# A two-layer decoder trunk on one core: the norm's sums one unit later, one mean by VectorE, and single PSUM tiles in two places

## The chip, the core and the metric

The kernel runs on one core of a Trainium2 chip. The metric is the device time of one execution in microseconds (us). The engines are named as the profile names them: PE (TensorE) with its weight loads PEld, DVE (VectorE), ACT (ScalarE), POOL (GpSimd), SP (SyncE, which here only issues DMAs).

## The reference

256 tokens of width 2048 in float32 pass two layers. Each layer is a mixer and a gated feed-forward net (FFN), each followed by a layer norm over a scaled residual:

```python
for i in range(DEPTH):                       # 2 layers
    if i < N_A_LAYERS:
        mix = pool_mixer(h, pool_w_in[i], pool_w_grp[i], pool_scale[i], pool_w_out[i])
    else:
        if i == N_A_LAYERS:                  # shared keys and values from the stream after layer 0
            k_shared = (h @ shared_w_k)...; v_shared = (h @ shared_w_v)...
        mix = dilated_attention(h, k_shared, v_shared, attn_w_q[j], attn_w_o[j])
    h = layer_norm(DEEPNORM_ALPHA * h + mix, ln1_g[i], ln1_b[i])
    ff = conv_ffn(h, ffn_w_up[i], ffn_conv_w[i], ffn_conv_b[i], ffn_w_down[i])
    h = layer_norm(DEEPNORM_ALPHA * h + ff, ln2_g[i], ln2_b[i])
```

`layer_norm` subtracts the mean over the 2048 features, divides by the root of the variance and applies a gain and an offset per feature.

## The kernel before

**Units.** All weights pass once through the core as blocks of 512 x 512 (128 partitions x 4 row chunks x 512 columns), 1 MB each, some of 384 rows. One block is one entry of the list `units`. `run_units` goes through that list: for unit i it first issues loads up to unit i + 5 and the splits up to unit i + 3 (`ahead`), then runs what `before[i]` holds, then emits the unit's matmuls, then the actions of `pending` that are due, then the unit's `post`, where it is the last of a group. `later(n, fn)` puts an action behind the matmuls of the n-th next unit. Each engine works through its own instructions in the order of emission, so this hand-written order decides what waits behind what.

**Splitting.** Weights and activations are float32. A block is split into a rounded part `wh` (ACT, line 99) and the rest `wl` (DVE, line 100), four buffers of each; a raw block has three buffers, so the load of unit u starts when unit u - 3 is split. The first four units are split in four pieces each. Activations are kept in tiles of quarters: `XC[q]` holds the high and the low part of quarter q of the features (512 of 2048), `H[q]` the float32 stream. The matmuls multiply high by high, high by low and low by high.

**PSUM.** One pool gives all accumulators: four tiles of two banks (`pair`); `bank` takes a pair's first half only. The framework puts in the semaphores. It orders the accesses of different engines to one PSUM tile.

**The start.** `x_quad(q)` transposes quarter q of x by eight matmuls into one pair, one bank for each half of the quarter, then for each half ACT copies the high part and DVE subtracts to get the low part; one ACT copy of both banks to `H[q]` follows in the unit after. Quarters 1 to 3 are transposed in the middle of units 0 to 2.

**The norm after the first FFN.** `add_last` multiplies by the down projection in four column groups c = 0 to 3; `resid_last` adds each group's result to `H[c]`. When H[0] is complete, a quarter of its mean-like sum is used as a shift (`shift`), which is taken off every quarter, so that the variance can be taken from sums of squares: H[0] by DVE in `one`, H[1] to H[3] by accumulating DMAs that POOL issues (`less`). `stats` and `folds` then sum each quarter and its square into `ST["S"]` and `ST["Q"]`; `xp(q)` makes `XP[q]`, the quarter times the gain and not yet normalised. `chain` has PE sum S and Q over the partitions (lines 429 and 430), then computes the inverse deviation and, one step per unit, normalises the quarters (`norm`), applies gain and offset (`affine`) and makes the high and low parts (`lo`, line 305) that become `XC[q]`.

**What follows that norm.** Twelve units for the first four heads: four units of keys, which read `XP[q]` and are corrected afterwards by the mean and deviation (`norm_evac`, two units behind the last of them), four units of queries, which read `XC[0]` to `XC[3]` in turn, four units of values. The order of `later` numbers in `chain` and in `qk_post` decides in which order these steps stand on ACT and DVE.

**The end of the attention.** `outputs(hq, ms)` multiplies two heads' values by their transposed probabilities into one pair, and ACT and DVE make the two parts that the output projection reads; for the last group of heads (hq = 3) they do so head by head.

Of the kernel before, what the change touches and what calls it, by code (L numbers as in the profile page):

```python
# [9 lines left out]
F32 = mybir.dt.float32  # L10
# [3 lines left out]
OP = mybir.AluOpType  # L14
# [3 lines left out]
T = 256  # L18
P = 128
# [13 lines left out]
def trunk(ctx: ExitStack, tc: tile.TileContext, x, pool_w_in, pool_w_grp, pool_scale, pool_w_out,  # L33
# [3 lines left out]
    V, A, PE = nc.vector, nc.scalar, nc.tensor  # L37
# [10 lines left out]
    def pair(nm):  # L48
        return psp.tile([P, 2, 512], F32, name=nm, tag="ps")

    def bank(nm):
        return pair(nm)[:, 0, :]

    def pairs(ps, n=4):
        return [(m, min(2, n - m), ps[m].both) for m in range(0, n, 2)]
# [16 lines left out]
    pending, before = [], {}  # L72
# [62 lines left out]
    def later(n, fn):  # L135
        if n == 0:
            fn()
        else:
            pending.append([n, fn])
# [158 lines left out]
    def w4(nm):  # L298
        return lnp.tile([P, 4, T], F32, name=nm, tag="w4")
# [15 lines left out]
    H, XC, XP, ST = {}, {}, {}, {}  # L315
    vec, cvec, gbx = [], [], {}
    ident = const.tile([P, P], F32, name="ident")
# [13 lines left out]
    def resid_last(c, first, lay, which, after):  # L331
        def post(ps):
            for m, n, p in pairs(ps):
                y = H[c][:, m:m + n, :]
                if first and c == 0:
                    V.scalar_tensor_tensor(y, y, ALPHA, p[:, :, :T], op0=OP.mult, op1=OP.add)
                else:
                    V.tensor_tensor(y, y, p[:, :, :T], OP.add)
                if c < 3:
                    V.tensor_tensor(y, y, p[:, :, T:], OP.add)  # L340
                else:
                    square(3, m)
            if c == 0:
                ST["w4"] = w4("fold")
                s = fold(H[0], None, "S0", F32R)
                later(1, lambda: shift(s, first, lay, which))
            elif c < 3:
                n = 3 if c == 1 and not first else 1
                later(n, lambda: stats(c))
                later(n + 1, lambda: xp(c, lay, which))  # L350
            else:
                folds(3)
                xp(3, lay, which)
                later(1, lambda: chain(ps[0], lay, which, after))
        return post

    def square(q, m):
        if m == 0:
            ST["sq"] = lnp.tile([P, 4, T], F32, name="sq", tag="sq")
        A.activation(ST["sq"][:, m:m + 2], H[q][:, m:m + 2], AF.Square)  # L360

    def fold(src, acc, nm, dt=F32):
        t2, t1 = ST["w4"][:, 0:2, :], ST["w4"][:, 2, :]
        V.tensor_tensor(t2, src[:, 0:2, :], src[:, 2:4, :], OP.add)
        if acc is None:
            t1 = lnp.tile([P, T], dt, name=nm, tag=nm[0])
        V.tensor_tensor(t1, t2[:, 0, :], t2[:, 1, :], OP.add)
        if acc is None:
            return t1
        V.tensor_tensor(acc, acc, t1, OP.add)  # L370
        return acc

    def folds(q):
        ST["S"] = fold(H[q], ST["S"], "S")
        ST["Q"] = fold(ST["sq"], ST["Q"], "Q")

    def stats(q):
        square(q, 0)
        square(q, 2)
        folds(q)  # L380

    def shift(s, first, lay, which):
        ps = bank("shift")
        PE.matmul(ps[:, :T], ones4, s, start=True, stop=True)
        if first:
            cs = ST["w4"][:, 3:4, :]
        else:
            cs = pools["ffn"].tile([P, 2, T], F32, name="cs", tag="xs", bufs=1)[:, 0:1, :]
        A.activation(cs[:, 0, :], ps[:, :T], AF.Copy, scale=-1.0)
        cb = cs.to_broadcast([P, 4, T])  # L390
        ST["S"] = ST["Q"] = None

        def one():
            V.tensor_tensor(H[0], H[0], cb, OP.add)
            if first:
                pre(1)
            stats(0)

        def two():
            xp(0, lay, which)  # L400
            if first:
                pre(2)
                pre(3)

        def pre(q):
            V.scalar_tensor_tensor(H[q], H[q], ALPHA, cb, op0=OP.mult, op1=OP.add)

        def less(q):
            nc.gpsimd.dma_start(H[q], cb, accum_op=OP.add)

        later(1, one)
        later(2, two)
        if not first:
            for q in (1, 2, 3):
                less(q)

    def xp(q, lay, which):
# [10 lines left out]
    def chain(ps, lay, which, after):  # L428
        PE.matmul(ps[:, :T], onesd, ST["S"], start=True, stop=True)
        PE.matmul(ps[:, T:], onesd, ST["Q"], start=True, stop=True)  # L430
        rm = lnp.tile([P, 4, T], F32, name="rm", tag="sq")
        rs, mr, var = rm[:, 0, :], rm[:, 1, :], rm[:, 2, :]
        ST["rs"], ST["mr"] = rm[:, 0:1, :], mr
        A.activation(rm[:, 3, :], ps[:, :T], AF.Square)
        V.tensor_tensor(var, ps[:, T:], rm[:, 3, :], OP.subtract)
        A.activation(var, var, AF.Sqrt, bias=epst)
        V.reciprocal(rs, var)
        V.tensor_tensor(mr, ps[:, :T], rs, OP.mult)
        mb, rb = rm[:, 1:2, :].to_broadcast([P, 4, T]), rm[:, 0:1, :].to_broadcast([P, 4, T])
        g0 = 32 * which  # L440

        def norm(q):
            V.tensor_tensor(H[q], H[q], rb, OP.mult)
            V.tensor_tensor(H[q], H[q], mb, OP.subtract)

        def affine(q):
            XC[q] = quad_tile("xc")
            for m in range(4):
                j = 4 * q + m
                A.activation(H[q][:, m, :], H[q][:, m, :], AF.Identity,  # L450
                             scale=vec[lay][:, g0 + j:g0 + j + 1], bias=vec[lay][:, g0 + 16 + j:g0 + 17 + j])
            A.copy(XC[q][:, :, 0, :T], H[q])

        def lo(q):
            lo_part(XC[q], H[q], 4)
            if after is not None:
                later((8, 11, 14, 17)[q], lambda: after(q))

        norm(0)
        for q in range(4):  # L460
            if q > 0:
                later(1 + q, lambda q=q: lo(q - 1))
            later(1 + q, lambda q=q: affine(q))
            if q < 3:
                later(1 + q, lambda q=q: norm(q + 1))
        later(5, lambda: lo(3))
# [69 lines left out]
    def x_quad(q, halves=(0, 1)):  # L536
        xin = XIN
        if halves[0] == 0:
            H[q] = hp.tile([P, 4, T], F32, name="h", tag="h")
            XC[q] = quad_tile("xc")  # L540
        if halves[0] == 0:
            ST["xT"] = pair("xT")
        both = ST["xT"]
        for half in halves:
            for kk in range(2):
                for t in range(2):
                    k = 2 * half + kk
                    PE.transpose(both[:, half, kk * T + t * P:kk * T + t * P + P], xin[q, t][:, k * P:(k + 1) * P],
                                 ident)
        for half in halves:  # L550
            pv2 = both[:, half, :].rearrange("p (k t) -> p k t", k=2)
            s = slice(2 * half, 2 * half + 2)
            A.copy(XC[q][:, s, 0, :T], pv2)
            V.tensor_tensor(XC[q][:, s, 1, :T], pv2, XC[q][:, s, 0, :T].bitcast(F32), OP.subtract)
        if halves[-1] == 1:
            before.setdefault(min(q + 1, 3), []).append(
                lambda: A.copy(H[q], both.rearrange("p b (k t) -> p (b k) t", k=2)))

    def add_in(g, mids=()):
        group(pool_w_in[0], rows4, 512 * g, 512, xsrcs, pool_post(g), mode="a" if g == 3 else "ab", mids=mids)  # L560
# [1 line left out]
    def add_grp(g):  # L562
# [12 lines left out]
             True, 0, 0, after=lambda q: to_tokens(q))  # L575
# [388 lines left out]
    qk, pr, oq, pT, vts = {}, {}, {}, {}, {}  # L964
# [140 lines left out]
    def outputs(hq, ms):  # L1105
        if ms[0] == 0:
            oq[hq] = quad_tile("o")
        vt = vts[hq]
        both = pair("o")
        for m in ms:  # L1110
            hd = slice(m * P, (m + 1) * P)
            ps = both[:, m % 2, :]
            t = pT.pop((hq, m))
            PE.matmul(ps[:, :T], vt[:, 0, hd], t[:, :T], start=True, stop=False)  # L1114
            PE.matmul(ps[:, P:T], vt[:, 1, hd], t[:, T:], start=False, stop=True)
        o = oq[hq][:, ms[0]:ms[0] + 2]
        for at in (slice(0, 1), slice(1, 2)) if hq == 3 else (slice(0, 2),):
            hi = o[:, at, 0, :T]
            A.copy(hi, both[:, at, :T])
            V.tensor_tensor(o[:, at, 1, :T], both[:, at, :T], hi.bitcast(F32), OP.subtract)  # L1120

    def v_group(hq):
        js = (0, 1, 2, 3)
# [18 lines left out]
    with tc.tile_pool(name="start", bufs=1) as stp:  # L1142
        one1 = stp.tile([P, P], F32, name="one1")
        for q in range(NQ):
            for t in range(2):
                XIN[q, t] = stp.tile([P, 512], F32, name=f"xin{q}{t}")
            halves = [slice(0, 256), slice(256, 512)] if q == 0 else [slice(0, 512)]
# [130 lines left out]
```

## Time and profile before

| | |
|---|---|
| median of 3 runs | 2023.74 us (2023.49 to 2025.34) |
| the profiled execution | 2024.98 us, its span 2023.2 us |
| instructions | 31428 |
| mean granted clock of PE | 0.999 |
| HBM read | 380.01 MB, 189 GB/s over the span |

The span runs from the first to the last instruction of the program. In the page's groups, in timelines and lists of waits, a line such as L100 is line 100 of the kernel; `out<-in` are the program's tile names; a bracket `[0.76 <-DVE xc L554]` is the time that the engine stood idle just before, and what ended it. Times in a timeline are us from the span's start, then the duration. An x and a number count instructions.

### The profile page before, as it was taken

The numbers are of one execution on the slowest core, as the hardware profiler recorded it, in microseconds if no ns is written. First come the engines' busy times: TensorE is split into PE (matmuls) and PEld (weight loads), VectorE is DVE, ScalarE is ACT, GpSimd is POOL, SyncE is SP. The second block draws the span as 40 slices with busy tenths as digits, with TensorE's granted clock in tenths as the row PEclk, the third lists the DMA queues.
The fourth block names the chain that finished last, engine by engine and source line by source line (L and its number), as shares of the span: only waits on it lengthen the run. The fifth ranks groups of instructions, "written<-read, shape, count | busy, mean of one in ns | idle before, by whom it ended". The sixth has DMA issues, their size and how long they took to land.

```text
span 2023.2 us, 31428 instructions
## 1 busy us (share of the span) xinstructions
PE 2011.6 (99%) x12742; PEld 1813.7 (90%) x12742; DVE 1728.5 (85%) x1822; ACT 1269.2 (63%) x1546; POOL 94.3 (5%) x154
## 2 busy tenths in 40 slices
PE   9999999999999999999999999999999999999999
PEld 8898988999899988888898988998899989989987
DVE  6868887999899999779796878787899899989898
ACT  5454686766766676656554444477767677667672
POOL 2000000000000000000000021000000000000000
PEclk9999999999999999999999999999999999999999
DMA  8565576676666767885565656557666757666765
GB/s 256 192 211 188 164 216 191 180 221 222 197 198 205 233 190 219 236 226 187 177 207 165 199 175 207 188 175 221 167 215 203 227 179 227 193 222 189 211 220 173
DMA packets 271825, 408.30 MB, mean 202 GB/s; under 512 B 74446, under 2 KB 86116, under 8 KB 271424
## 3 DMA queue, kind: packets, MB, share of 16 engines
q1 hardware_dynamic: 259488, 388.93, 59.1%
q0 software_dynamic: 11760, 16.70, 5.5%
q8 instruction: 100, 1.64, 0.3%
q10 hardware_dynamic: 432, 0.66, 0.1%
q14 instruction: 45, 0.37, 0.1%
HBM read 380.01 MB, written 2.10 MB: 189 GB/s over the span
## 4 chain that ended last, share of the span: by engine, by line
PE 98%; DVE 1%; DMA 0%; issue 0%; ACT 0%; SPq 0%; DVEq 0%
PE acc L180 44%; PE acc L181 22%; PE s L246 3%; PE s L244 3%; PE s L245 3%; PE acc L185 3%; PE t L246 2%; PE t L244 2%; PE t L245 2%; PE acc L184 2%; PE acc L183 2%; PE t L255 2%; PE t L257 2%; PE t L256 2%; PE s L1064 0%; PE o L1114 0%
## 5 line engine op out<-in xcount | busy, mean ns | idle before, releaser
L180 PE MATMUL acc<-xc,wh 128*128 128x512 f32 x3264 | 1151.8, 396 | 0.0
L181 PE MATMUL acc<-xc,wl 128*128 128x256 f32 x3264 | 916.0, 281 | 0.0
L100 DVE TENSOR_TENSOR wl<-raw,wh 128x2048 fp32r<-128x2048 f32 (+2 forms) x305 | 657.1, 2163 | 174.9 <-ACT wh L99 170.3
L180 PEld LDWEIGHTS acc<-xc,wh 128*128 128x128 f32 x3264 | 616.0, 189 | 143.3
L99 ACT CAST wh<-raw 128x2048 fp32r<-128x2048 f32 (+2 forms) x305 | 548.7, 1805 | 170.1 <-PE acc L180 70.4
L181 PEld LDWEIGHTS acc<-xc,wl 128*128 128x128 f32 x3264 | 615.4, 189 | 0.1
L113 ACT CAST wh<-raw 128x1024 fp32r<-128x1024 f32 x142 | 148.4, 1052 | 194.5 <-DVE raw L122 175.3
L114 DVE TENSOR_TENSOR wl<-raw,wh 128x1024 fp32r<-128x1024 f32 x142 | 169.4, 1221 | 11.2 <-ACT wh L113 11.2
L121 DVE TENSOR_TENSOR wl<-raw,wh 128x1536 fp32r<-128x1536 f32 x71 | 124.5, 1754 | 6.7 <-ACT wh L119 5.7
L119 ACT CAST wh<-raw 128x1536 fp32r<-128x1536 f32 x71 | 104.9, 1477 | 35.4 <-PE acc L180 28.2
L287 POOL DMA_DIRECT2D ht<-w x48 | 41.3, 1014 | 1446.7 <-DVE ht L877 722.1
L246 PE MATMUL t<-wh,g 128*128 128x256 f32 x376 | 105.7, 281 | 0.0
L244 PE MATMUL t<-wh,g 128*128 128x256 f32 x376 | 105.6, 281 | 0.0
L245 PE MATMUL t<-wl,g 128*128 128x256 f32 x376 | 105.4, 280 | 0.0
L620 ACT ACTIVATE c<-u,cv 128x256 f32<-128x256 f32 x172 | 89.5, 592 | 23.1 <-DVE f L682 16.6
L246 PE MATMUL s<-wh,xs 128*128 128x256 f32 x344 | 96.2, 280 | 0.0
L244 PE MATMUL s<-wh,xs 128*128 128x256 f32 x344 | 96.1, 279 | 0.0
L245 PE MATMUL s<-wl,xs 128*128 128x256 f32 x344 | 96.0, 279 | 0.0
L124 DVE TENSOR_TENSOR raw<-raw 128x1024 f32<-128x1024 f32 x71 | 87.0, 1225 | 2.4
L625 ACT ACTIVATE a<-u,cv 128x256 f32<-128x256 f32 x172 | 73.4, 499 | 11.9 <-DVE g L692 11.9
L611 ACT COPY u<-acc 128x512 f32<-128x512 f32 x84 | 46.9, 573 | 47.4 <-PE acc L181 47.1
L625 ACT ACTIVATE u<-u,cv 128x256 f32<-128x256 f32 x172 | 73.4, 499 | 0.0
(337 smaller groups left out, 3445.2 us busy)
## 6 DMA issues: line engine op xcount, KB each, us to landing
raw<-in_ffn_w_up_dram SPq DMA_DIRECT2D x160, 1024.0 KB, 5.2
raw<-in_ffn_w_down_dram SPq DMA_DIRECT2D x80, 1024.0 KB, 5.2
raw<-in_pool_w_out_dram SPq DMA_DIRECT2D x16, 1024.0 KB, 5.0
raw<-in_shared_w_k_dram SPq DMA_DIRECT2D x16, 1024.0 KB, 5.1
raw<-in_attn_w_q_dram SPq DMA_DIRECT2D x16, 1024.0 KB, 5.1
raw<-in_shared_w_v_dram SPq DMA_DIRECT2D x16, 1024.0 KB, 5.2
raw<-in_attn_w_o_dram SPq DMA_DIRECT2D x16, 1024.0 KB, 5.4
ht<-w POOLq DMA_DIRECT2D x50, 256.0 KB, 5.3
```

Source lines behind the costliest of these rows:

```text
L99: A.copy(wh[i][:, s], r[:, s])
L100: V.tensor_tensor(wl[i][:, s], r[:, s], wh[i][:, s].bitcast(F32), OP.subtract)
L113: A.copy(h[:, :, n], r[:, :, n])
L114: V.tensor_tensor(l[:, :, n], r[:, :, n], h[:, :, n].bitcast(F32), OP.subtract)
L119: A.copy(hs, rs)
L121: V.tensor_tensor(ls, rs, hs.bitcast(F32), OP.subtract)
L180: PE.matmul(ps[m].ap, h[:, k, c], q[:, k, :, :T], start=st, stop=False)
L181: PE.matmul(ps[m][:, :T], l[:, k, c], q[:, k, 0, :T], start=False, stop=sp)
L244: PE.matmul(to, xh, h[:, k, n], start=opens and kk == 0, stop=False)
L245: PE.matmul(to, xh, l[:, k, n], start=False, stop=False)
L246: PE.matmul(to, xl, h[:, k, n], start=False, stop=ends and kk == 1)
L625: A.activation(to[:, m, :], u[:, m, i:i + T], AF.Copy, scale=cv[:, i, j:j + 1])
```

## The change

- `resid_last`: for the norm after the first FFN, the only one with `first` false, `chain` is put behind the second unit after the sums are made, not behind the first. The steps that `chain` places by `later` move with it.
- `shift`: there, the shift of H[1] is added by a DVE instruction in `one`, behind that of H[0]; `less` issues DMAs for H[2] and H[3] only.
- `x_quad`: each half of a quarter gets a PSUM tile of its own (a pair of which one bank is used). Transposes, copy and subtraction are emitted half by half. The copies to H are two for each quarter and stand at the start of unit q, not of unit q + 1 (3 at most).
- `outputs`: the last two heads of the last group get a PSUM tile each, and are copied and subtracted as soon as the head's matmuls are emitted. The first two heads of that group are copied and subtracted together, as those of the other groups are.

```diff
@@ resid_last
-                later(1, lambda: chain(ps[0], lay, which, after))
+                later(1 if first else 2, lambda: chain(ps[0], lay, which, after))
@@ shift
             if first:
                 pre(1)
+            else:
+                V.tensor_tensor(H[1], H[1], cb, OP.add)
             stats(0)
...
         if not first:
-            for q in (1, 2, 3):
+            for q in (2, 3):
                 less(q)
@@ x_quad
-        if halves[0] == 0:
-            ST["xT"] = pair("xT")
-        both = ST["xT"]
         for half in halves:
+            ps = bank("xT")
             for kk in range(2):
                 for t in range(2):
                     k = 2 * half + kk
-                    PE.transpose(both[:, half, kk * T + t * P:kk * T + t * P + P], xin[q, t][:, k * P:(k + 1) * P],
-                                 ident)
-        for half in halves:
-            pv2 = both[:, half, :].rearrange("p (k t) -> p k t", k=2)
+                    PE.transpose(ps[:, kk * T + t * P:kk * T + t * P + P], xin[q, t][:, k * P:(k + 1) * P], ident)
+            pv2 = ps.rearrange("p (k t) -> p k t", k=2)
             s = slice(2 * half, 2 * half + 2)
             A.copy(XC[q][:, s, 0, :T], pv2)
             V.tensor_tensor(XC[q][:, s, 1, :T], pv2, XC[q][:, s, 0, :T].bitcast(F32), OP.subtract)
-        if halves[-1] == 1:
-            before.setdefault(min(q + 1, 3), []).append(
-                lambda: A.copy(H[q], both.rearrange("p b (k t) -> p (b k) t", k=2)))
+            before.setdefault(q, []).append(lambda s=s, pv2=pv2: A.copy(H[q][:, s, :], pv2))
@@ outputs
-        both = pair("o")
+        last = hq == 3 and ms[0] == 2
+        both = None if last else pair("o")
         for m in ms:
             hd = slice(m * P, (m + 1) * P)
-            ps = both[:, m % 2, :]
+            ps = bank("o") if last else both[:, m % 2, :]
...
+            if last:
+                hi = oq[hq][:, m, 0, :T]
+                A.copy(hi, ps[:, :T])
+                V.tensor_tensor(oq[hq][:, m, 1, :T], ps[:, :T], hi.bitcast(F32), OP.subtract)
-        o = oq[hq][:, ms[0]:ms[0] + 2]
-        for at in (slice(0, 1), slice(1, 2)) if hq == 3 else (slice(0, 2),):
-            hi = o[:, at, 0, :T]
-            A.copy(hi, both[:, at, :T])
-            V.tensor_tensor(o[:, at, 1, :T], both[:, at, :T], hi.bitcast(F32), OP.subtract)
+        if not last:
+            o = oq[hq][:, ms[0]:ms[0] + 2]
+            A.copy(o[:, :, 0, :T], both[:, :, :T])
+            V.tensor_tensor(o[:, :, 1, :T], both[:, :, :T], o[:, :, 0, :T].bitcast(F32), OP.subtract)
```

## The prediction

> **What bounds the kernel now.** I read the page's busy shares first, then its chain, then the list of TensorE's waits, then stretches and timelines around those waits.
>
> ```profile
> PE 2011.6 (99%) x12742; PEld 1813.7 (90%) x12742; DVE 1728.5 (85%) x1822; ACT 1269.2 (63%) x1546; POOL 94.3 (5%) x154
> PE 98%; DVE 1%; DMA 0%; issue 0%; ACT 0%; SPq 0%; DVEq 0%
> ```
>
> TensorE (PE) is busy nearly all the time and carries 98% of the chain that ended last. The change takes no matmul away, so it can only move the stretches in which PE stands still. These are few:
>
> ```profile
> PE acc L429 <- DVE S L370: 2.6, 1, 2.6
> PE acc L430 <- DVE Q L370: 0.8, 1, 0.8
> PE acc L185 <- DVE wl L100: 0.9, 3, 0.3
> PE acc L180 <- DVE o L1120: 0.5, 2, 0.2
> ```
>
> The first two are the statistics matmuls of the norm after the first FFN (`chain`), the third is the start (units 1 to 3), the fourth the end of the attention. All three places are touched. I call the units after the first FFN K0 to K3 (keys), Q0 to Q3 (queries), V0 and so on (values). Cutting the trace at their first matmuls gives stretches (columns: us, then busy time and count of PE, PEld, DVE, ACT, POOL, then granted clock, DMA share, GB/s):
>
> ```profile
> 924.73:930.50 5.77, 5.77 (x50) 5.72 (x48) 5.77 (x7) 0.00 (x0) 0.00 (x0) 1.00 0.45 148
> 930.50:935.45 4.95, 1.52 (x7) 0.88 (x5) 4.78 (x11) 4.40 (x8) 0.00 (x0) 0.93 0.74 255
> 935.45:942.64 7.19, 7.19 (x51) 7.10 (x49) 6.58 (x8) 4.25 (x5) 0.00 (x0) 0.81 0.39 128
> 942.64:948.43 5.79, 5.79 (x50) 5.79 (x49) 5.72 (x5) 4.33 (x6) 0.00 (x0) 1.00 0.21 48
> 948.43:954.18 5.75, 5.75 (x51) 5.75 (x49) 5.26 (x5) 5.47 (x7) 0.00 (x0) 1.00 0.68 230
> 954.18:971.06 16.88, 16.88 (x98) 14.73 (x97) 15.11 (x13) 10.75 (x16) 0.00 (x0) 1.00 0.56 192
> 971.06:976.71 5.65, 5.65 (x34) 4.92 (x33) 3.17 (x4) 5.04 (x6) 0.00 (x0) 1.00 0.27 102
> ```
>
> They are K0; the wait with the four statistics matmuls; K1; K2; K3; Q0 to Q2; Q3. K1 took 7.19 us at a mean clock of 0.81 where K0 took 5.77 at 1.00: after the wait PE ran at half speed for a while, which cost another 1.42 us. The four matmuls by themselves need some 0.9 us, so this place loses about 4.95 - 0.9 + 1.42 = 5.5 us.
>
> **The norm, the larger term.** Two edits. The first moves the mean's add onto H[1] from a POOL DMA to VectorE (DVE):
>
> ```profile
> DVE h L338 <- DMA h<-cs: 4.7, 1, 4.7
> 893.01 1.22 DVE L394 TENSOR_TENSOR h<-h,cs 128x1024 f32<-128x1024 f32 x1
> ```
>
> One DMA leaves POOL's queue of three, and DVE gets a second add like the one at 893.01: 1.2 us more work, 4.7 us of waiting less, so everything behind it on DVE (splits, folds, sums) runs some 3.5 us earlier. The H[2] and H[3] DMAs have one fewer ahead of them. This alone would take the sums to about 930 us, near PE's arrival at 930.50, and leave a stall of about 1 us.
>
> The second edit runs `chain` behind K1 instead of K0. Then the 3.5 us lead buys nothing more, since the sums are done 5 us before they are wanted. PE goes from K0 straight into K1: K1 is 930.50 to 936.27 (5.77), the four matmuls end at 937.13, K2 and K3 (5.79, 5.75) end at 948.67. There PE wants Q0, 5.5 us earlier than before. But Q0 reads XC[0], and its last piece, `lo(0)`, comes out of the norm. The rows of that path before:
>
> ```profile
> 936.04 0.39 ACT L434 ACTIVATE rm<-acc 128x256 f32<-128x256 f32 x1 [0.32 <-PE acc L430]
> 936.45 1.28 ACT L436 ACT_TABLE_LOAD   x1
> 938.88 0.51 ACT L436 ACTIVATE rm<-rm,epst 128x256 f32<-128x256 f32 x1 [1.15 <-DVE rm L435]
> 939.43 1.75 DVE L437 RECIPROCAL rm<-rm 128x256 f32<-128x256 f32 x1 [0.58 <-ACT rm L436]
> 951.29 1.22 DVE L305 TENSOR_TENSOR xc<-h,xc 128x1024 fp32r<-128x1024 f32 x1
> 957.02 1.22 DVE L305 TENSOR_TENSOR xc<-h,xc 128x1024 fp32r<-128x1024 f32 x1
> 962.75 1.22 DVE L305 TENSOR_TENSOR xc<-h,xc 128x1024 fp32r<-128x1024 f32 x1
> 967.88 1.22 DVE L305 TENSOR_TENSOR xc<-h,xc 128x1024 fp32r<-128x1024 f32 x1
> 969.02 0.68 DVE L474 TENSOR_TENSOR k<-acc,rm 128x512 f32<-128x512 f32 x1
> 974.57 4.49 DVE L100 TENSOR_TENSOR wl<-raw,wh 128x2048 fp32r<-128x2048 f32 x2 [2.44 <-ACT wh L99]
> ```
>
> From the reciprocal to the end of `lo(0)` went 952.51 - 939.43 = 13.1 us, with DVE nearly full: normalise H[0], split a block, normalise H[1], split a block, `lo(0)`. The same list stands behind the moved chain; only the blocks are Q1 and Q2 instead of Q0 and Q1, as all of the chain has moved one unit against the splits. The reciprocal is now held by PE and ACT: 937.13 + 0.39 + 1.28 + 0.51 = 939.3 us, the same moment as before. So `lo(0)` ends at 952.4 us as before. Before, PE asked for it at 954.18 and found it done; now it asks at 948.67 and waits 3.7 us. Of 5.5 us gained, 1.8 are left.
>
> DVE then makes one `lo` every 5.73 us (951.29, 957.02, 962.75) and PE uses one every 16.88 / 3 = 5.63: Q1 starts at about 958.2 and Q2 at 963.9, each with 0.1 us of waiting. `lo(3)` is different. Before it stood ahead of the evacuation of the keys (L474 on), in the same step; one unit later it stands behind it and behind V1's split. From the evacuation's start to the start of that split took 974.57 - 969.02 = 5.55 us, because ScalarE (ACT) ends the evacuation, only then makes wh, and DVE waits for it. From the end of `lo(2)` at 963.97: + 5.55 + 2.2 (half of the 4.49 for two splits) + 1.2 = 973.0 us. PE asks at 963.9 + 5.63 = 969.6 and waits 3.4 us. Q3 thus starts at 973.0 where it started at 971.06: **+1.9 us**, and all that follows is late by that, since no later wait of PE is long enough to absorb it.
>
> What the clock makes of these stalls is the unknown term. Bounds: nothing, or the 1.42 us of K1 after each, 2.8 in all. Delay in Q0 is partly hidden, since the evacuation and V1's split lag it by less; behind Q3 nothing hides it. I take once **+1.4**, by K1's row: the stalls are as long as the one that row follows.
>
> [...]
>
> **The start.** PE's stretches of units 1, 2, 3, ahead of them the second half of unit 0 (columns: us, PE busy and count, clock, DMA share, GB/s):
>
> ```profile
> 12.36:15.28 2.92, 2.92 (x27) 1.00 1.06 397
> 15.28:22.42 7.14, 6.85 (x58) 1.00 1.04 384
> 22.42:29.54 7.12, 6.86 (x58) 1.00 0.66 222
> 29.54:36.56 7.02, 6.67 (x50) 1.00 0.42 115
> 11.64 0.98 PE L548 MATMUL xT<-ident,xin 128*128 128x128 f32 x7 [0.37 <-DMA xin<-in_x_dram]
> 12.66 0.59 ACT L553 CAST xc<-xT 128x512 fp32r<-128x512 f32 x1 [2.71 <-PE xT L548]
> 14.01 0.59 ACT L553 CAST xc<-xT 128x512 fp32r<-128x512 f32 x1 [0.76 <-DVE xc L554]
> 15.23 2.49 DVE L100 TENSOR_TENSOR wl<-raw,wh 128x512 fp32r<-128x512 f32 x4
> 18.70 1.04 PE L548 MATMUL xT<-ident,xin 128*128 128x128 f32 x8
> ```
>
> Half a unit without a wait takes 2.92 us, and eight transposes take 0.8 (1.04 less the overlap). So unit 1 loses 7.14 - 5.84 - 0.8 = 0.5, unit 2 as much, unit 3 (no transposes, all four wl pieces at once) 7.02 - 5.84 = 1.2: 2.2 us together. Cause: the first copy waits for all eight transposes, and the second copy, of another bank, waited 0.76 us for DVE's read of the first half, both in one tile. With a tile for each half the first copy starts four transposes (0.4 us) sooner and the second doesn't wait for DVE (0.7): wl begins about 1.1 us before 15.23, earlier than PE asks. I take **-2.1**. [...] The copies to H become eight half copies and move one unit forward. They cost nothing while ACT is idle there: it idled 2.71 us before 12.66, so two copies of 0.6 for H[0] end near 11.1, and the PSUM slots that they free are wanted at 11.64, when x arrives. If that cover fails, about 0.6 us comes back.
>
> **The last heads.**
>
> ```profile
> 1234.77 0.37 ACT L1119 CAST o<-o 128x256 fp32r<-128x256 f32 x1 [2.64 <-PE o L1115]
> 1235.18 0.42 DVE L1120 TENSOR_TENSOR o<-o 128x256 fp32r<-128x256 f32 x1 [0.72 <-ACT o L1119]
> 1235.64 0.37 ACT L1119 CAST o<-o 128x256 fp32r<-128x256 f32 x1 [0.49 <-DVE o L1120]
> 1236.04 0.42 DVE L1120 TENSOR_TENSOR o<-o 128x256 fp32r<-128x256 f32 x1 [0.44 <-ACT o L1119]
> ```
>
> Copy, subtract, copy, subtract stand in a row in one tile, and PE waits after each subtraction. With a tile for each head the first turn runs beside the second head's matmuls, and the second starts at 1234.77, where the first did. One turn goes: 1235.64 - 1234.77 = **-0.9** (bounds -0.5, PE's wait as listed, and -1.0). The first two heads of this group go back to one copy and one subtraction for both, which PE is not listed as waiting for: 0.
>
> **The sum.** The profiled execution took 2024.98 us (span 2023.2, 1.8 around it): 2024.98 + 1.9 + 1.4 - 2.1 - 0.9 = 2025.3. That execution lies 1.2 above the median, 2023.74, and beside the slowest run, 2025.34; a half clock that comes in some runs only would make such a gap. For the median I take off half of it: **2024.7 us**, +0.05%. About 0.2% (4 us) is what a measurement of this kernel can tell from no change.
>
> **Rivals.** *The clock stays full through both stalls*: 1.4 less, 2023.3. For it: only one of the four places where PE waits in this trace has a lower clock behind it. [...] *The clock drops after both* (slower): 2.8 instead of 1.4, or more if the half speed lasts twice as long as K1's; 2026 to 2029. [...] *No late reader*: if XC[0] and XC[3] were ready in time, the whole 5.5 would be gained and with it the start and the heads: 2024.98 - 5.5 - 3.0 = 2016.5. Against it is the 13.1 us of full DVE, which nothing in the change shortens. *The change does not do what it says at the start*: if transfers (DMA share 1.04 in unit 1) or the copies hold the pieces, 2.1 comes back: 2026.8.
>
> **How the numbers follow.** Forecast 0.43, clock full 0.27, clock halved twice 0.15, no late reader 0.09, start without gain 0.06. The forecast's own range is 2023 to 2026.5. The range 2021.0 to 2028.3 takes in all but no late reader and the top of the second. Faster by over 0.2% (under 2019.7) is the no-late-reader case, 0.09; slower (over 2027.8) about half of the clock halved twice and a little of the last, 0.11; within, 0.80.
>
> **What would show it.** Right: no wait at L429 and L430; new waits of PE, both on DVE's xc (L305), at Q0 of 3 to 4 us and at Q3 of about 3.4; DVE's H[1] add without a DMA wait; no waits at L185 of the start; one short wait or none at L1120. Wrong: PE passing Q0 or Q3 without a wait, a wait for xT slots or transfers before 40 us, or a half clock lasting longer than 3.4 us.

## The result: 0.19% slower, a loss of about 4 us

| | median | runs |
|---|---|---|
| before | 2024.23 us | 13 (2021.59 to 2026.66) |
| changed | 2028.20 us | 13 (2026.65 to 2030.02) |

The ratio is 1.0019, 95% interval 1.0012 to 1.0026. The interval leaves out 1, so the change costs about 4 us: a small loss, but a real one. The profiled execution of the changed kernel took 2028.55 us with a span of 2026.8; the one before had 2024.98 and 2023.2, 3.6 us less in both.

TensorE's list of waits in the changed kernel (us in total, times, longest; two lines of the first 7 us, 1.1 and 0.4 us in both traces, are left out):

```profile
PE acc L180 <- DVE xc L305: 7.0, 2, 4.0
PE acc L183 <- ACT wh L99: 1.9, 1, 1.9
PE acc L185 <- DVE wl L100: 0.2, 1, 0.2
```

Gone are the waits at the statistics matmuls (3.4 us), at the start's wl (0.9, now 0.2) and behind the last heads (0.5). New are two waits for `lo`, 7.0 us together. The one at L183 is in unit 0 and goes back to a transfer; it is told of below.

The same stretches as before, cut at the first matmuls of K0, K1, K2 (the four statistics matmuls end K1's stretch), K3, its end, Q0, Q1, Q2, its end, Q3 and V0 (us, busy time and count of PE, PEld, DVE, ACT, POOL, granted clock, DMA share, GB/s):

```profile
923.01:928.78 5.77, 5.77 (x50) 5.77 (x49) 5.63 (x8) 3.08 (x8) 0.00 (x0) 1.00 0.89 300
928.78:935.21 6.43, 6.43 (x55) 6.35 (x53) 6.40 (x8) 3.42 (x2) 0.00 (x0) 1.00 0.23 64
935.21:941.19 5.98, 5.98 (x50) 5.95 (x49) 3.89 (x5) 3.98 (x4) 0.00 (x0) 1.00 0.87 332
941.19:946.94 5.75, 5.75 (x50) 5.71 (x48) 5.69 (x4) 4.43 (x6) 0.00 (x0) 1.00 0.18 40
946.94:951.05 4.11, 0.16 (x2) 0.03 (x1) 3.66 (x4) 4.08 (x7) 0.00 (x0) 1.00 0.59 207
951.05:958.29 7.24, 7.24 (x32) 6.25 (x33) 7.17 (x6) 4.39 (x6) 0.00 (x0) 0.76 0.61 200
958.29:963.90 5.61, 5.61 (x34) 4.84 (x33) 4.33 (x4) 5.06 (x8) 0.00 (x0) 1.00 0.33 120
963.90:969.51 5.61, 5.61 (x34) 4.87 (x32) 3.10 (x7) 3.62 (x5) 0.00 (x0) 1.00 0.50 180
969.51:972.80 3.29, 0.26 (x3) 0.03 (x1) 3.29 (x3) 1.90 (x1) 0.00 (x0) 0.88 0.09 7
972.80:981.24 8.44, 8.44 (x33) 7.25 (x33) 2.74 (x2) 0.59 (x1) 0.00 (x0) 0.64 0.74 248
```

K0 to K3 now run without a gap at full clock. Then PE stands for 4.11 us with 0.16 busy, while DVE and ACT are nearly full. Q0 follows at a clock of 0.76 and takes 7.24 us where 5.61 is the pace. Behind Q2 PE stands again, 3.29 us, and Q3 takes 8.44 us at 0.64.

Why `lo(0)` and `lo(3)` come when they do, in DVE's timeline:

```profile
937.84 1.75 DVE L439 RECIPROCAL rm<-rm 128x256 f32<-128x256 f32 x1 [1.40 <-ACT rm L438]
949.69 1.22 DVE L305 TENSOR_TENSOR xc<-h,xc 128x1024 fp32r<-128x1024 f32 x1
955.43 1.22 DVE L305 TENSOR_TENSOR xc<-h,xc 128x1024 fp32r<-128x1024 f32 x1
962.53 1.22 DVE L305 TENSOR_TENSOR xc<-h,xc 128x1024 fp32r<-128x1024 f32 x1
963.67 0.68 DVE L476 TENSOR_TENSOR k<-acc,rm 128x512 f32<-128x512 f32 x1
969.23 2.29 DVE L100 TENSOR_TENSOR wl<-raw,wh 128x2048 fp32r<-128x2048 f32 x1 [2.44 <-ACT wh L99]
971.43 1.22 DVE L305 TENSOR_TENSOR xc<-h,xc 128x1024 fp32r<-128x1024 f32 x1
```

From the reciprocal to the end of `lo(0)` are 950.91 - 937.84 = 13.1 us, the length that this path had before. Behind `lo(2)` (962.53) come the evacuation of the keys (from 963.67), 2.44 us in which DVE waits for ACT's wh, V1's split, and only then `lo(3)` (971.43), which lets Q3 start.

The other two places. The start, units 1 to 3 (us, PE busy and count, clock, DMA share, GB/s), and the last two heads:

```profile
15.81:22.39 6.58, 6.58 (x59) 1.00 0.98 342
22.39:28.98 6.59, 6.59 (x59) 1.00 0.77 279
28.98:34.84 5.86, 5.86 (x50) 1.00 0.63 184
1238.62 0.37 ACT L1115 CAST o<-o 128x256 fp32r<-128x256 f32 x1 [3.87 <-PE o L1112]
1239.02 0.43 DVE L1116 TENSOR_TENSOR o<-o 128x256 fp32r<-128x256 f32 x1 [1.95 <-ACT o L1115]
1239.27 0.37 ACT L1115 CAST o<-o 128x256 fp32r<-128x256 f32 x1 [0.28 <-PE o L1112]
1239.68 0.43 DVE L1116 TENSOR_TENSOR o<-o 128x256 fp32r<-128x256 f32 x1 [0.23 <-ACT o L1115]
```

The three units took 7.14, 7.12 and 7.02 us and now take 6.58, 6.59 and 5.86: 2.25 us gained. At the heads the second copy no longer waits for the first subtraction but for its own matmuls (0.28 behind PE).

**The account.** First matmuls in the two traces: unit 4 at 36.56 and 34.84, V0 at 976.71 and 981.24, PE's next wait behind the heads 0.87 us shorter. So: start -1.7, norm +6.25 (4.53 + 1.72), heads -0.9, sum +3.6, the difference of the spans. Of the 2.25 us gained at the start 0.5 was lost ahead of it: unit 1 began at 15.81 and not 15.29. ACT shows why, first before, then changed:

```profile
7.97 1.98 ACT L99 CAST wh<-raw 128x512 fp32r<-128x512 f32 x3 [0.31 <-DMA raw<-in_pool_w_in_dram]
9.40 1.97 ACT L99 CAST wh<-raw 128x512 fp32r<-128x512 f32 x3 [2.03 <-DMA raw<-in_pool_w_in_dram]
```

The second piece of the first weights landed 1.4 us later than in the execution before. The change need not be the cause: in e1 and e2 below, which have the old start, ACT stands 1.98 and 2.08 us for the same transfer. Unit 1 began at 17.60 and 17.34 there, later still, with the clock also at 0.50 for 3.41 us in unit 0 (from 11.47 and from 11.93). So traces are compared below from unit 4 on: from there to V0 went 940.15 us before and 946.40 in the changed kernel.

### The profile page after: what moved, and what is told of

It reads as the page before. It is cut to its first block, busy times and chain, and to the rows that moved or that the text cites. A ratio compares the mean times of both kernels' runs of the same rounds, so it can differ in the third digit from the quotient of the medians.

```text
span 2026.8 us, 31425 instructions
## 1 busy us (share of the span) xinstructions
PE 2011.5 (99%) x12742; PEld 1814.1 (90%) x12742; DVE 1729.0 (85%) x1822; ACT 1269.4 (63%) x1549; POOL 93.1 (5%) x153
## 4 chain that ended last, share of the span: by engine, by line
PE 98%; DVE 1%; ACT 1%; DMA 0%; issue 0%; SPq 0%; DVEq 0%; ACTq 0%
PE acc L180 43%; PE acc L181 22%; PE s L246 3%; PE s L244 3%; PE s L245 3%; PE acc L184 3%; PE acc L185 3%; PE acc L183 3%; PE t L246 2%; PE t L244 2%; PE t L245 2%; PE t L255 2%; PE t L257 2%; PE t L256 2%; PE s L1060 0%; PE o L1111 0%
```

## The experiments

The theory was that running `chain` one unit later costs more than its wait was worth, and that the other three edits pay. The rival was that the added VectorE instruction or the interplay of the edits costs. Each ratio is to the kernel before, measured beside the experiment (medians 2024.85 us for e1 to e4, 2024.25 for e5 and e6). The changed kernel was measured at another time, so a distance to it rests more on the stretches from unit 4 to V0 than on the medians.

**e1: H[1]'s shift by VectorE, alone.**

```diff
             if first:
                 pre(1)
+            else:
+                V.tensor_tensor(H[1], H[1], cb, OP.add)
             stats(0)
-            for q in (1, 2, 3):
+            for q in (2, 3):
```

> The kernel before with one edit: the shift of H[1] by VectorE, chain still one unit after the sums. Theory (chain one unit later is what costs; the mean's add pays): VectorE's 4.7 us wait for the DMA goes, the sums are ready about 3.4 us sooner, TensorE waits at the statistics matmuls for about 1 us and not 3.4, the clock stays full; 3.4 to 4.8 us faster than before, ratio 0.9977 to 0.9983. Rival (the added VectorE instruction costs as much as the DMA wait, and the loss comes from it): no gain, ratio 1.000 or over.

2020.68 us, ratio 0.9986 (0.9978 to 0.9995). PE's list of waits has no statistics matmul any more:

```profile
PE acc L183 <- ACT wh L99: 1.8, 1, 1.8
PE acc L185 <- DVE wl L100: 1.1, 4, 0.3
PE acc L180 <- DVE o L1122: 0.5, 2, 0.3
```

From unit 4 to V0 went 935.31 us, 4.8 less than before. The wait at the norm is gone wholly where about 1 us was expected to stay. This edit alone does what the second one was added for.

**e2: `chain` two units behind, alone.**

```diff
-                later(1, lambda: chain(ps[0], lay, which, after))
+                later(1 if first else 2, lambda: chain(ps[0], lay, which, after))
```

> The kernel before with one edit: chain two units after the sums, H[1] still by DMA. Theory: no wait at the statistics matmuls, but VectorE is later than in the changed kernel by about 2.3 us when the norm begins, so TensorE waits at the first query unit for 5 to 6 us and at the fourth for over 3, with the clock at half behind both; 7 to 10 us slower than before, ratio 1.0035 to 1.005. Rival (the later chain pays and the add costs): as before or faster, ratio 1.000 or under.

2032.87 us, ratio 1.0044 (1.0030 to 1.0057). The stretches of both waits and of Q0 and Q3 behind them:

```profile
950.20:956.68 6.48, 0.15 (x2) 0.03 (x1) 6.02 (x6) 6.42 (x8) 0.00 (x0) 0.79 0.56 168
956.68:964.25 7.57, 7.57 (x33) 6.56 (x33) 7.50 (x6) 4.38 (x6) 0.00 (x0) 0.73 0.59 202
975.50:978.75 3.25, 0.23 (x2) 0.03 (x1) 3.25 (x3) 1.90 (x1) 0.00 (x0) 0.87 0.08 8
978.75:987.17 8.42, 8.42 (x33) 7.23 (x33) 2.74 (x2) 0.58 (x1) 0.00 (x0) 0.65 0.70 248
```

Two waits, 6.48 and 3.25 us, each with slow matmuls behind it. Unit 4 to V0: 949.08, 8.9 more than before. The loss is this edit's; the other norm edit hides 2.7 us of it in the changed kernel (949.08 - 946.40).

**e3: the two edits of PSUM tiles, alone** (`x_quad` and `outputs` as in the change, `resid_last` and `shift` as before).

> The kernel before with the two edits of PSUM tiles (start and last heads), the norm as before. Theory: the waits at line 185 of the start and after the last heads go, 1.7 to 2.2 and 0.9 us; 2.6 to 3.1 us faster, ratio 0.9985 to 0.9987. Rival (the start waits for transfers in any case): 0.9 us, ratio 0.9996.

2021.62 us, ratio 0.9984 (0.9975 to 0.9992). Units 1 to 3 take 19.01 us (15.79 to 34.80) against 21.28 before, so 2.27 gained, and the heads 0.87. The rival is out: transfers do not hold units 1 to 3, although the DMA share is 1.01 in unit 1. Not all of the gain is the edits': in the profiled execution the norm, which e3 does not touch, took 0.97 us less than before (939.18 from unit 4 to V0 against 940.15), with 1.9 us of waiting at L429 and not 2.6. So the norm's time can differ by about 1 us between two executions whose norm is the same.

**e4: the changed kernel with `chain` back at one unit.**

```diff
-                later(1 if first else 2, lambda: chain(ps[0], lay, which, after))
+                later(1, lambda: chain(ps[0], lay, which, after))
```

> The changed kernel with chain back at one unit after the sums. Theory: the sum of the two gains, 3.4 to 4.8 and 2.6 to 3.1 us: 6 to 8 us faster than before, ratio 0.996 to 0.997, and some 10 us faster than the changed kernel. Rival (the edits need each other): within 1 us of the changed kernel.

2017.34 us, ratio 0.9970 (0.9958 to 0.9981): faster than both kernels, 10.9 us under the changed one (10.8 from unit 4 to V0: 935.59 against 946.40). K0, the four statistics matmuls, K1 and Q0 to V0:

```profile
922.83:928.61 5.78, 5.78 (x51) 5.78 (x49) 5.64 (x8) 3.08 (x8) 0.00 (x0) 1.00 0.89 307
928.61:929.61 1.00, 0.94 (x6) 0.51 (x5) 0.96 (x4) 1.00 (x1) 0.00 (x0) 1.00 0.71 272
929.61:935.59 5.98, 5.98 (x50) 5.95 (x49) 5.40 (x6) 4.38 (x5) 0.00 (x0) 1.00 0.22 54
947.14:969.97 22.83, 22.83 (x130) 19.73 (x129) 18.54 (x17) 15.81 (x21) 0.00 (x0) 1.00 0.55 184
```

The statistics take 1.00 us in all, and the four query units 22.83, 5.71 each, at full clock.

**e5: the changed kernel with the evacuation of the first keys one unit later**, so that it stands behind `lo(3)` as it did before.

```diff
-            later(2 if hq == 0 and nm == "k" else 0, lambda: evac(ps))
+            later(3 if hq == 0 and nm == "k" else 0, lambda: evac(ps))
```

> The changed kernel with one number changed: the evacuation of the first keys three units behind them, not two, which puts it behind lo(3) again. Theory (the wait at the fourth query unit comes from lo(3) standing behind the evacuation and the split that waits for it): the wait at the first query unit stays at about 4 us with its half clock, the one at the fourth goes with its half clock (3.2 and 2.8 us); 5 to 6 us faster than the changed kernel, ratio to before 0.998 to 1.000. Rival (VectorE simply has too much to do between the first and the fourth query unit, in whatever order): a wait of 1 to 3 us stays there, 0 to 3 us faster than the changed kernel.

2023.28 us, ratio 0.9994 (0.9985 to 1.0002). Q2 to Q3 and Q3 to V0, behind the unchanged first wait:

```profile
948.05:952.16 4.11, 0.16 (x2) 0.03 (x1) 3.67 (x4) 4.08 (x7) 0.00 (x0) 1.00 0.62 211
952.16:959.39 7.23, 7.22 (x32) 6.22 (x33) 7.16 (x6) 4.38 (x6) 0.00 (x0) 0.76 0.60 195
965.00:970.71 5.71, 5.71 (x35) 4.99 (x34) 3.68 (x3) 2.03 (x3) 0.00 (x0) 1.00 0.59 188
970.71:976.38 5.67, 5.67 (x35) 4.93 (x33) 3.17 (x7) 4.09 (x6) 0.00 (x0) 1.00 0.49 178
```

DVE's rows show `lo(3)` ahead of the evacuation:

```profile
969.24 1.22 DVE L305 TENSOR_TENSOR xc<-h,xc 128x1024 fp32r<-128x1024 f32 x1
970.38 0.68 DVE L476 TENSOR_TENSOR k<-acc,rm 128x512 f32<-128x512 f32 x1
```

The second wait is gone with its slow unit, 5.9 us from unit 4 to V0 (940.48 against 946.40). So it was the place of `lo(3)` in the queue, not the amount of VectorE's work.

**e6: the changed kernel with matmuls that nobody reads in both waits.**

```diff
+    def fill(n, q):
+        ps = bank("fill")
+        for i in range(n):
+            PE.matmul(ps[:, :T], ones4, q[:, 0, 0, :T], start=True, stop=True)
...
+        if hq == 0:
+            before.setdefault(len(units), []).append(lambda: fill(28, XP[3]))
+            before.setdefault(len(units) + 3, []).append(lambda: fill(24, XC[2]))
         group(attn_w_q[0], rows4, 512 * hq, 512, xsrcs, qk_post("q", hq))
```

> The changed kernel with matmuls that nobody reads put into TensorE's two waits, 28 ahead of the first query unit and 24 ahead of the fourth, so that TensorE is idle for under 1 us at each. Theory (the clock halves because TensorE stands idle, and costs 1.6 us in the first query unit, in part hidden, and 2.8 in the fourth): the granted clock stays at 1.00, the units behind the waits take 5.6 us, lo(0) and lo(3) come at about the same time; 3 to 4 us faster than the changed kernel, ratio to before about 1.000. Rival (the slow units are slow for another reason than TensorE's idling, such as VectorE's and ScalarE's accesses): no gain, or slower by what the added matmuls delay.

2023.87 us, ratio 0.9997 (0.9988 to 1.0006), 4.3 us under the changed kernel. The two waits, now filled, and Q0 and Q3:

```profile
946.08:950.19 4.11, 3.45 (x31) 3.27 (x29) 3.67 (x4) 4.08 (x7) 0.00 (x0) 1.00 0.59 214
950.19:955.92 5.73, 5.73 (x32) 4.91 (x33) 5.70 (x5) 4.39 (x6) 0.00 (x0) 1.00 0.55 185
967.26:970.51 3.25, 3.15 (x27) 2.95 (x25) 3.25 (x3) 1.91 (x1) 0.00 (x0) 1.00 0.01 4
970.51:976.26 5.75, 5.75 (x33) 5.00 (x34) 2.84 (x2) 0.59 (x1) 0.00 (x0) 1.00 0.93 310
```

The waits are as long as ever (4.11, 3.25), but the clock stays at 1.00 and Q0 and Q3 take 5.73 and 5.75 instead of 7.24 and 8.44. The slow units were slow because PE had idled, and that cost 4.1 us (946.40 - 942.28 from unit 4 to V0).

## Why the prediction was right, and which term was not

The time, 2028.2, lies 0.1 us inside the top of the range, and the change is within 0.2%, as forecast. That it lies inside is in part luck: the forecast's 2024.7 was 3.5 us short, the time is outside the forecast's own range of 2023 to 2026.5, and the range reached it only by taking in a rival. In the traces the terms sum to +3.6 us where the forecast's sum to +0.3. Of the 3.3 us between them 2.7 are the clock's and 0.4 the start's.

- **Where the stall goes**: as argued. Both new waits are at Q0 and Q3 on `lo`, 4.1 and 3.3 us for 3.7 and 3.4. The 13.1 us path was measured again at 13.1.
- **The shift of Q3 by +1.9**: with the clock held at full (e6) Q3 starts 936.53 us behind unit 4 where it started 934.50 behind before: +2.0. With the clock as it was, +3.46.
- **The clock, +1.4**: this is the step that failed. I counted one of the two waits, and held that Q0's delay would be partly hidden. Both waits were followed by a low clock. Q0's 1.6 us was hardly hidden: V0's split needs the buffers of Q0's block, so ACT waited for the slow Q0 (the rows below, of the changed kernel and of e6, where Q0 is not slow). Counted from unit 4, the evacuation, V1's split and `lo(3)` all came some 1.3 us later than in e6, and Q3 1.4 (3.46 - 2.03). And behind Q3 the half speed cost 8.44 - 5.65 = 2.8, twice K1's 1.42. The term was 4.1 us by e6; the rival "the clock drops after both" is what happened, and its 2026 to 2029 held the time. Shorter waits than these two had a low clock behind them as well: in the kernel before those of 2.6 and 0.8 us at L429 and L430 (0.50 from 934.79 to 938.20), in e3 those of 1.9 and 0.8 us (0.50 from 931.73 to 935.14).

```profile
958.38 1.91 ACT L99 CAST wh<-raw 128x2048 fp32r<-128x2048 f32 x1 [1.87 <-PE acc L180]
955.96 1.92 ACT L99 CAST wh<-raw 128x2048 fp32r<-128x2048 f32 x1 [0.33 <-PE acc L180]
```

- **The start, -2.1, and the heads, -0.9**: 2.25 and 0.87, each also in e3 (2.27 and 0.87). At the start 0.5 was lost again ahead of unit 1.
- **VectorE's add, 3.5 us less waiting**: seen. The add of H[1] (first row below) follows that of H[0] without a wait, and the last sum (second row, and before in the third) ends 3.6 us sooner, counted from unit 4: 929.38 - 34.84 against 934.73 - 36.56. But I gave it too little by itself. A stall of about 1 us was left over in my sum, and 0.1 was (1.00 us for the statistics in e4, some 0.9 of it their own). With it the later chain had nothing left to gain, and the change paid for it.

```profile
892.43 1.22 DVE L398 TENSOR_TENSOR h<-h,cs 128x1024 f32<-128x1024 f32 x1
928.96 0.42 DVE L370 TENSOR_TENSOR Q<-Q,fold 128x256 f32<-128x256 f32 x1
934.30 0.43 DVE L370 TENSOR_TENSOR Q<-Q,fold 128x256 f32<-128x256 f32 x1
```

Two of the three signs of being wrong that the prediction names did come: a wait for a transfer before 40 us (1.9 us at L183, above) and a half clock longer than 3.4 us (6.83 us at Q3, below; in the kernel before it lasted 3.41, from 934.79).

The wait at Q3 was 3.29 us, with 0.26 us of it busy, and the clock fell, as it did at the wait of 3.25 us in e2. The half clock began inside the wait, at 972.04, when PE had idled for 2.27 us (since 969.77). With the term of 0 of the rival whose clock stays full the norm would have been priced 4.1 us too low.

## What to carry to other kernels

When a step is moved later to spare a wait, list not only who stood in that wait but who reads the step's last output, and count the queue ahead of that output in the new order; here the same 3 us of wait came back at the first reader and once more at the fourth, which had been overtaken by an evacuation. Price a stall of TensorE with the slow matmuls behind it: each of the five waits of 3.25 to 6.48 us in the changed kernel, e2 and e5 came with 3.41 or 6.83 us at a granted clock of 0.50. And try edits one by one: the one that removed the cause (a DMA wait on the path) gains 4.8 us alone, and the one that moved the symptom costs, alone (8.9 us) as beside the others (10.8).

## What the runs showed of the chip that I had not expected

- The half clock lasted 3.41 us behind Q0's wait and 6.83 us, twice that, behind Q3's, so the longer loss stood behind the shorter wait (4.11 and 3.29 us). The rows below cut the changed kernel's trace where the clock changed (columns as in the stretches above). Q3's half clock began 0.76 us ahead of its first matmul, and the 3.42 us with that idling in it were followed by 3.41 more at half. In e2 the two half clocks lasted 6.83 us each, in e3 and e5 3.41. What decides between the two lengths was not varied.

```profile
951.56:954.97 3.41, 3.41 (x12) 2.92 (x11) 3.38 (x3) 2.37 (x5) 0.00 (x0) 0.50 0.79 299
968.63:972.04 3.41, 1.14 (x7) 0.72 (x5) 2.81 (x2) 2.46 (x2) 0.00 (x0) 1.00 0.00 0
972.04:975.46 3.42, 2.66 (x8) 2.31 (x9) 2.81 (x2) 0.00 (x0) 0.00 (x0) 0.50 0.78 251
975.46:978.87 3.41, 3.41 (x13) 2.92 (x12) 0.00 (x0) 0.57 (x1) 0.00 (x0) 0.50 1.00 317
978.87:982.28 3.41, 3.41 (x20) 2.91 (x19) 0.91 (x2) 0.85 (x3) 0.00 (x0) 1.00 0.13 51
```

- Filling a wait with useless matmuls gained 4.3 us in the median, although each added matmul is work on the busiest engine (PE, 99% of the changed kernel's span).
- Unit 1 began between 14.98 us (e6) and 17.60 us (e1) in the profiled executions, with the loads issued in the same order. In the three latest (e1, e2, and e5 with 16.85) the clock was at 0.50 for 3.41 us in unit 0, behind waits at L183 of 1.8, 2.0 and 1.5 us; in the changed kernel a wait of 1.9 us there had no half clock behind it. What makes the first weights land so unevenly was not tried.
